# The last layer's ConvGLU up projection by seven half-size products instead of eight, in rounds of four feature tiles

## The chip, the cores and the metric

The kernel runs on one core of a Trainium2 chip. The metric is device time of one execution in microseconds, the median of several runs. A core has a matrix engine (TensorE, PE in the profile; its weight loads are listed apart as PEld), VectorE (DVE), ScalarE (ACT), GpSimd (POOL), and a sync engine (SP) that here issues the large DMAs. Each engine takes its instructions in the order in which they stand in its own queue; semaphores make one engine wait for another. Matrix products accumulate in PSUM (eight banks of 128x512 fp32); everything else lives in SBUF.

## The reference: what is computed

Two layers over 512 latent tokens and 256 context tokens of 1024 features, in fp32. Layer 0 is windowed attention, layer 1 is a bidirectional gated linear recurrence (HGRN2). Each layer ends in a ConvGLU, the part that matters here:

```
hx2 = rms_norm(x, norm2_g) * (1 + sc2) + sh2          # 512 x 1024
gate, val = split(hx2 @ w_up, 2)                      # w_up 1024 x 5632, two halves of 2816
y = (silu(dwconv3(gate, conv_w, conv_b)) * val) @ w_down   # w_down 2816 x 1024
x = x + g2 * y
```

`dwconv3` mixes three neighbouring tokens per feature. In layer 0 the ConvGLU runs over latent and context tokens, in the last layer over the 512 latent tokens alone.

## The kernel before

Activations lie transposed: features on the partitions, tokens along the free axis. All products are fp32 by splitting: an operand is written as a rounded part and a remainder (`wh`, `wl` for weights; index 0 and 1 for activations), and three products wh·high, wh·low, wl·high are added in PSUM, so each logical 128x128 block costs three matmuls. A weight block of 128x512 costs one ScalarE copy (`wh`) and one VectorE subtraction (`wl`).

`norm` is folded in: the up projection runs on x·(gain) and its result is multiplied by a per-token factor `R` (1/rms), which is computed beside the first products. Two more columns carry the adaLN shift, so the 512 tokens become 514 columns.

**The up projection** works by feature tile `ft` (22 of them, 128 features of gate and the same 128 of val: "a pair"). Two ways are in the file:

- `gate_plain` (used in the last layer before the change): gate and val one after the other, each as two column halves of 256 and 258 in two PSUM banks (`pd`); 2 x 8 x 3 x 2 = 96 matmuls a pair. Four weight blocks of 128x512 are split (lines 117 and 118). VectorE reads each PSUM half times `R` into `G` (gate) or `gg` (val): four operations (line 924).
- `gate_pair` (used in layer 0): the 2x2 block product [gate; val] = W x [first half of tokens, second half] by the seven-product scheme of Strassen and Winograd. Rows of W are gate/val against the two halves of the 1024 input features; seven sums of weight quarters (`load_pair`, lines 128 to 160: four VectorE sums, line 136, and seven splits, lines 140 and 141) meet seven sums of activation quarters (`hs[0..6]`, made once by `halves` and `combos`). Each product has 4 x 3 = 12 matmuls, 84 a pair, into three banks `pZ`, `pY`, `pV`; ScalarE copies four intermediate results out, VectorE makes five 128xhalf operations (lines 937 and 938), GpSimd multiplies `gg` by `R` (line 938).

After either, the convolution, the silu and the product with val run on VectorE and ScalarE (lines 995 to 1008) and give `g`, split into two parts.

**The down projection** accumulates over a round of feature tiles in PSUM (`dn`), in four parts `dp` of 256 output features: two banks of 128x512 each, 2 x nf x 3 matmuls for a round of nf tiles. At a part's end VectorE adds each bank to the residual `xl` (line 1035). `ROUNDS` gives the round sizes: (8, 7, 7) in the last layer. Before a round's four parts only one pair of the next round has been computed (`ahead`); the rest follow after the parts.

What sets the order: the program is written as above, but a list scheduler orders each engine's instructions; weight splits are given priority (`W_AHEAD = 180`). Weight operands rotate through four pools (`operand`): one with four buffers and three with two. Raw weights arrive in two buffers `wr`, by DMAs from SP's queue.

Ahead of the last ConvGLU stands `hgrn_out`, the recurrence's output projection (`ho` matmuls, 512 columns): its evictions (line 907) give `xl`, and from it the scaled operand `hn` (lines 362, 363) and the sum of squares for `R` (line 527) are made. At the end `done1` transposes the finished `xl` tiles (`xo`) and four DMAs write the output.

Of the kernel before, what the change touches and what calls it, by code (L numbers as in the profile page):

```python
# [16 lines left out]
P = 128  # L17
# [13 lines left out]
ROUNDS = ((3, 3, 4, 4, 3, 5), (8, 7, 7))  # L31
# [41 lines left out]
class Kernel:  # L73
# [16 lines left out]
    def load_raw(self, parts):  # L90
        raw = self.wp.tile([P, 2048], F32, tag="wr", name="wr")
# [7 lines left out]
    def load_w(self, parts, cols=False):  # L99
# [3 lines left out]
        raw, n = self.load_raw(parts)  # L103
# [425 lines left out]
    def row_factor(self, acc, lat_only, tmp, pp, tag, width, R, sh, dg):  # L529
# [18 lines left out]
        if R.shape[1] > TW:  # L548
            nc.vector.memset(R[:, TW:], sh)

# [358 lines left out]

    def gate_plain(self, ft, ops, hn, G, gg, R, rows, half, tmp, bank):  # L910


        nc = self.nc
        act = lambda k: (hn[:, 0, k], hn[:, 1, k])
        cols = ((0, 256), (256, C0))
        for j, dst in enumerate((G[:, 1:1 + C0], gg)):
            ps = [bank("pd")[:, 0:hi - lo] for lo, hi in cols]
            for _ in self.mm_steps(ops[j], range(KT), act, [(o, lo) for o, (lo, _) in zip(ps, cols)]):
                pass
            for _ in rows:  # L920
                pass

            for o, (lo, hi) in zip(ps, cols):
                nc.vector.tensor_tensor(dst[:, lo:hi], o, R[:, lo:hi], op=ALU.mult)

# [44 lines left out]
    def ffn(self, l, hs, R, rows, lat_only, tmp, acp, bk, gp, done, side=None):  # L970
        nc, a = self.nc, self.a
        wup, wdn = a["ffn_w_up"][l], a["ffn_w_down"][l]
        half = C0 // 2 if lat_only else hs[0].shape[3]
# [11 lines left out]
        def up(ft):  # L985

            ws_ = [self.wcols(wup, ft * P, P), self.wcols(wup, DFF + ft * P, P)]
            ops = self.load_w(ws_) if lat_only else self.load_pair(ws_, tmp)
# [8 lines left out]
            nc.vector.tensor_scalar(cb[:, :nv], G[:, 1 + SH:1 + SH + nv], ws[:, ft:ft + 1], cw[:, 66 + ft:67 + ft], op0=ALU.mult, op1=ALU.add)  # L997
# [13 lines left out]
        f0, late, ahead = 0, None, []  # L1011
        for r, nf in enumerate(ROUNDS[l]):
            gt = ahead + [up(ft) for ft in range(f0 + len(ahead), f0 + nf)]

            ahead = [up(f0 + nf)] if f0 + nf < NFF else []
            if side and r < 5:
                next(side, None)
            for dp in range(KT // 2):
# [8 lines left out]
                part = dp == 0 and not ahead  # L1027
# [435 lines left out]
```

## Time and profile before

| | |
|---|---|
| median of 3 runs | 1857.48 us (1855.71 to 1858.05) |
| the profiled execution: its time, its span | 1855.84 us, 1854.0 us |
| PE busy over the span | 1795.1 us, 97% |
| VectorE busy | 1213.7 us, 65% |
| last ConvGLU: first up matmul to the end | 1464.04 to 1854.0 us |
| of it: VectorE busy between 1464 and 1806 us | 185.43 us of 342 |
| granted TensorE clock, mean | 0.993 |

"Span" is the time between the first and the last instruction on the core, the run's time has a little around it. A busy engine is one with an instruction in flight; matmuls overlap, so their single durations are longer than the distance from one to the next. The same holds to a smaller degree for VectorE. The chain of waits follows the end of the program back to what released each step; its pieces show where PE itself was the reason.

### The profile page before, as it was taken

How to read it: one execution, taken by the hardware profiler on the slowest of the kernel's cores; microseconds unless marked ns; L12 is line 12 of the kernel's file. 1: busy time of each engine (PE TensorE's matmuls, PEld its weight loads, DVE VectorE, ACT ScalarE, POOL GpSimd, SP SyncE). 2: the span in 40 equal slices, each digit the busy share in tenths (PEclk: the TensorE clock that was granted, in tenths of full speed). 3: DMA queues.
4: the chain of work that ended last, by engine and by line, in shares of the span. 5: the costliest groups of instructions: out<-in, count | busy, mean ns of one | idle time of the engine just before them, and what ended most of it. 6: DMA issues, size and time to landing. Idle time of an engine off the chain costs nothing.

```text
span 1854.0 us, 32305 instructions
## 1 busy us (share of the span) xinstructions
PE 1795.1 (97%) x13326; PEld 1573.2 (85%) x13326; DVE 1213.7 (65%) x2273; ACT 754.4 (41%) x1478; POOL 201.6 (11%) x203
## 2 busy tenths in 40 slices
PE   5999999998999999999999999999998999999998
PEld 4986776787888988888998888888996799899997
DVE  5576676467878686767777666677765665365462
ACT  4355555465533443433454333333332433233332
POOL 1233333101100000000001110111110000000000
PEclk9999999999999999999999999999999999999999
DMA  9204104232343433333413222121220332332321
GB/s 309 69 24 151 55 24 157 82 103 91 103 121 97 128 123 114 100 106 103 128 52 97 58 58 58 36 57 36 58 69 24 91 92 92 102 97 87 91 83 66
DMA packets 204416, 166.43 MB, mean 90 GB/s; under 512 B 5149, under 2 KB 198254, under 8 KB 199150
## 3 DMA queue, kind: packets, MB, share of 16 engines
q1 hardware_dynamic: 196608, 160.47, 28.2%
q10 hardware_dynamic: 7662, 3.92, 0.7%
q8 instruction: 104, 1.70, 0.4%
q14 instruction: 42, 0.34, 0.1%
HBM read 162.27 MB, written 2.10 MB: 89 GB/s over the span
## 4 chain that ended last, share of the span: by engine, by line
PE 89%; DVE 4%; DMA 4%; issue 1%; ACT 1%; POOL 0%; SPq 0%; ACTq 0%; POOLq 0%; DVEq 0%
PE dn L170 15%; PE pd L170 14%; PE pZ L188 8%; PE pf L170 8%; PE pV L188 4%; PE pjq L610 4%; PE pv L170 4%; PE ao L170 4%; PE ho L170 3%; PE pq L170 3%; PE pv L836 3%; PE pt L828 2%; PE pgate L170 2%; PE ada L309 2%; PE pY L188 2%; PE kv L610 2%
## 5 line engine op out<-in xcount | busy, mean ns | idle before, releaser
L117 ACT ACTIVATE wh<-wr 128x512 fp32r<-128x512 f32 (+2 forms) x328 | 194.9, 608 | 467.7 <-DMA wr<-in_ffn_w_up 76.7
L118 DVE TENSOR_TENSOR wl<-wr,wh 128x512 fp32r<-128x512 f32 (+2 forms) x328 | 218.6, 674 | 132.3 <-ACT wh L117 131.7
L170 PE MATMUL dn<-g,wh 128*128 128x512 f32 (+1 forms) x1056 | 263.2, 357 | 0.0
L170 PE MATMUL pd<-hn,wh 128*128 128x256 f32 (+1 forms) x1408 | 227.6, 284 | 1.8 <-issue 1.8
L170 PEld LDWEIGHTS dn<-g,wh 128*128 128x128 f32 x1056 | 175.3, 189 | 29.5 <-DVE g L1008 0.3
L170 PEld LDWEIGHTS pd<-hn,wh 128*128 128x128 f32 x1408 | 194.5, 190 | 3.2 <-issue 3.0
L188 PE MATMUL pZ<-hs,wh 128*128 128x386 f32 x704 | 183.0, 342 | 1.8 <-ACT t L941 1.1
L170 PE MATMUL dn<-g,wl 128*128 128x512 f32 (+1 forms) x528 | 159.3, 356 | 0.0
L140 ACT ACTIVATE wh<-wr 128x512 fp32r<-128x512 f32 x132 | 82.4, 630 | 163.7 <-PE pZ L188 35.7
L170 PE MATMUL pd<-hn,wl 128*128 128x256 f32 x704 | 141.9, 283 | 0.0
L188 PEld LDWEIGHTS pZ<-hs,wh 128*128 128x128 f32 x704 | 127.4, 189 | 12.5 <-issue 5.9
L188 PE MATMUL pZ<-hs,wl 128*128 128x386 f32 x352 | 119.0, 342 | 3.9 <-DVE wl L141 3.9
L141 DVE TENSOR_TENSOR wl<-wr,wh 128x512 fp32r<-128x512 f32 x132 | 96.1, 734 | 40.7 <-ACT wh L140 39.5
L170 PE MATMUL pf<-hn,wh 128*128 128x512 f32 (+1 forms) x512 | 118.6, 347 | 2.9 <-DVE xc L1035 1.9
L170 PEld LDWEIGHTS pd<-hn,wl 128*128 128x128 f32 x704 | 109.2, 190 | 0.0
L1035 DVE SCALAR_TENSOR_TENSOR xl<-dn,mod,xl 128x512 f32<-128x512 f32 x72 | 53.8, 747 | 72.2 <-PE dn L170 71.9
L170 PEld LDWEIGHTS dn<-g,wl 128*128 128x128 f32 x528 | 87.6, 188 | 14.8
L938 POOL TENSOR_TENSOR gg<-gg,R 128x772 f32<-128x772 f32 x22 | 45.0, 2047 | 460.1 <-DVE gg L937 447.2
L188 PE MATMUL pV<-hs,wh 128*128 128x386 f32 x352 | 92.0, 341 | 2.1 <-DVE hs L384 1.6
L170 PEld LDWEIGHTS pf<-hn,wh 128*128 128x128 f32 x512 | 80.3, 191 | 15.7 <-DVE xc L1035 2.2
L610 PE MATMUL pjq<-wh,hn 128*128 128x256 f32 x384 | 77.8, 290 | 0.0
L188 PEld LDWEIGHTS pZ<-hs,wl 128*128 128x128 f32 x352 | 66.1, 188 | 8.9 <-DVE wl L141 6.4
(302 smaller groups left out, 3762.9 us busy)
## 6 DMA issues: line engine op xcount, KB each, us to landing
wr<-in_ffn_w_up SPq DMA_DIRECT2D x88, 512.0 KB, 5.2
wada<-in_ada_w SPq DMA_DIRECT2D x40, 1024.0 KB, 4.8
wr<-in_hgrn_w_in SPq DMA_DIRECT2D x40, 512.0 KB, 4.2
ar<-in_ada_w SPq DMA_DIRECT2D x32, 256.0 KB, 7.2
wr<-in_ffn_w_down SPq DMA_DIRECT2D x8, 896.0 KB, 4.7
wr<-in_attn_w_in SPq DMA_DIRECT2D x6, 1024.0 KB, 8.3
wr<-in_ffn_w_down SPq DMA_DIRECT2D x12, 384.0 KB, 3.4
wr<-in_attn_w_out SPq DMA_DIRECT2D x8, 512.0 KB, 5.6
```

The source lines that it names most:

```text
L117: nc.scalar.activation(wh, src, AF.Copy)
L118: nc.vector.tensor_tensor(wl, src, f(wh), op=ALU.subtract)
L140: nc.scalar.activation(ops[i][0], src, AF.Copy)
L141: nc.vector.tensor_tensor(ops[i][1], src, f(ops[i][0]), op=ALU.subtract)
L170: nc.tensor.matmul(o, lhsT=wt, rhs=at[:, t0:t0 + o.shape[1]], start=(first and n == 0 and i == 0), stop=(last and n == len(ks) - 1 and i = ...
L188: self.nc.tensor.matmul(ps, lhsT=wt, rhs=at, start=(first and k == 0 and i == 0), stop=(k == nk - 1 and i == 2), skip_group_check=not first)
L309: nc.tensor.matmul(ps[32 * j:32 * j + 32, 0:512], lhsT=self.cs[:, k, :], rhs=raw[:, j * 512:(j + 1) * 512], start=(k == 0), stop=(k == KT ...
L610: nc.tensor.matmul(out, lhsT=x, rhs=y[:, wk], start=(start and k == 0 and j == 0), stop=(stop and k == KT - 1 and j == 2))
L828: nc.tensor.transpose(pt[:, j * P:(j + 1) * P], pr[j][:, b * P:(b + 1) * P], self.ident)
L836: nc.tensor.matmul(pv[a * HD:(a + 1) * HD, 0:256], lhsT=V[:, tl, g, :], rhs=pT[:, a * 256:(a + 1) * 256], start=(b == 0), stop=(b == len(t ...
L938: times = lambda eng, o, x, y: eng.tensor_tensor(o, x, y, op=ALU.mult)
L1035: nc.vector.scalar_tensor_tensor(x[:, d], o, self.modc(l, v, 5, d), x[:, d], op0=ALU.mult, op1=ALU.add)
```

## The change

The last layer's ConvGLU uses `gate_pair` as layer 0 does (`gate_plain` goes away): half = 258 columns, 516 in all, the last two columns zero. For it `hgrn_out` no longer makes `hn`; it makes the seven activation sums `hs` with `halves` and `combos`, five of them tile by tile and the last two at its end. The rounds become (4, 4, 4, 4, 4, 2). The next round's pairs are all computed within this round, one ahead of each of the four parts of the down projection. Down weights get a raw buffer pool of their own (`wd`, two of 128x1024). Two 1-column VectorE operations per pair move to ScalarE, in both layers. The output staging tile takes a buffer of the pool of `g`.

```diff
-ROUNDS = ((3, 3, 4, 4, 3, 5), (8, 7, 7))
+ROUNDS = ((3, 3, 4, 4, 3, 5), (4, 4, 4, 4, 4, 2))
...
-            ops = self.load_w(ws_) if lat_only else self.load_pair(ws_, tmp)
+            ops = self.load_pair(ws_, tmp)
...
-            (self.gate_plain if lat_only else self.gate_pair)(ft, ops, hs, G, gg, R, rows, half, tmp, bank)
-            nc.vector.tensor_copy(ap(G[:, 0:1], 0, (TW + 1, nv)), G[:, 1 + SH:1 + SH + nv])
+            self.gate_pair(ft, ops, hs, G, gg, R, rows, half, tmp, bank)
+            nc.scalar.activation(ap(G[:, 0:1], 0, (TW + 1, nv)), G[:, 1 + SH:1 + SH + nv], AF.Copy)
...
-        f0, late, ahead = 0, None, []
+        f0, late = 0, None
+        gt = [up(ft) for ft in range(ROUNDS[l][0])]
         for r, nf in enumerate(ROUNDS[l]):
-            gt = ahead + [up(ft) for ft in range(f0 + len(ahead), f0 + nf)]
-
-            ahead = [up(f0 + nf)] if f0 + nf < NFF else []
...
+            coming = list(range(f0 + nf, f0 + nf + (*ROUNDS[l], 0)[r + 1]))
+            ahead = []
             for dp in range(KT // 2):
+                if len(ahead) < len(coming) and (lat_only or dp == 0):
+                    ahead.append(up(coming[len(ahead)]))
...
             f0 += nf
+            gt = ahead + [up(ft) for ft in coming[len(ahead):]]
...
+            some.append(self.combos(self.halves(1, 1, dp, 258, True, tmp, ("y0", "y1"), 4), dp, hs))
+            next(some[-1])
             for d in (dp, dp + 4):
-                self.scaled(1, 1, d, hn, True)
                 self.square_acc(d, acc, True, tmp, "sg", first=(d == 0))
+        for rest in some:
+            for _ in rest:
+                pass
```

The scheduler's result at two places. First VectorE at the start of the last ConvGLU, from the last eviction of the output projection (`xl<-ho`) on. Names: `wl` a weight remainder, `hn3` and `hs3` the activation operands, `acc2` the sum of squares, `rv` and `dg` the steps to `R`, `G` the gate tile, `y` the scaled token halves. Before, from that eviction to the first PSUM result:

```order
L907 SCALAR_TENSOR_TENSOR xl_4315<-ho_15256,mod1_124,xl_4315 128x512
L978 SCALAR_TENSOR_TENSOR wsum_15338<-par_111 128x22
L118 TENSOR_TENSOR wl_15505<-wr_15493,wh_15504 128x512
L979 TENSOR_TENSOR wsum_15338<-wsum_15338,par_111 128x22
L363 SCALAR_TENSOR_TENSOR hn3_15114<-xl_4315,gs1_126,hn3_15114 128x512
L527 TENSOR_TENSOR acc2_15118<-acc2_15118,sq_15314 128x512
L118 TENSOR_TENSOR wl_15771<-wr_15767,wh_15770 128x512
L118 TENSOR_TENSOR wl_15638<-wr_15630,wh_15637 128x512
L440 TENSOR_SCALAR rv_15418<-nss_15412 128x4
L541 TENSOR_TENSOR dg_15421<-cst_64,rs_15417 128x512
L924 TENSOR_TENSOR G_15360<-pd_15362,R2_15317 128x256
```

Now, the end of the same stretch; 17 operations of VectorE stand between the last eviction and the first row:

```order
L440 TENSOR_SCALAR rv_15516<-nss_15510 128x4
L922 TENSOR_TENSOR G_15464<-t_15469,pY_15467 128x258
L136 TENSOR_TENSOR wr_15428<-wr_15428 128x512
L141 TENSOR_TENSOR wl_15610<-wr_15593,wh_15609 128x512
L396 TENSOR_TENSOR y_15355<-y_15355 128x258
L396 TENSOR_TENSOR y_15351<-y_15355,y_15351 128x258
L384 TENSOR_TENSOR hs3_15114<-y_15355,hs3_15114 128x258
L141 TENSOR_TENSOR wl_15441<-wr_15428,wh_15440 128x512
L141 TENSOR_TENSOR wl_15600<-wr_15593,wh_15599 128x512
L384 TENSOR_TENSOR hs3_15114<-y_15351,hs3_15114 128x258
L541 TENSOR_TENSOR dg_15571<-cst_64,rs_15515 128x512
L141 TENSOR_TENSOR wl_15439<-wr_15428,wh_15438 128x512
```

The operand was complete with one operation of line 363, four rows after the eviction; now the last part of `hs3` stands 28 rows after it, among weight sums and splits of the first two pairs, and the first pair's last split stands behind it.

Second PE in a middle round. Before, at the change from the first round's pairs to its down parts (`g` is a finished feature tile, `wh`/`wl` behind it the down weights):

```order
L170 MATMUL pd_16525<-hn3_15114,wl_16468 128x256
L170 MATMUL pd_16526<-hn3_15114,wl_16468 128x258
L170 MATMUL dn_16607<-g_15490,wh_16591 128x512 x2
L170 MATMUL dn_16607<-g_15490,wl_16592 128x512
L170 MATMUL dn_16607<-g_15627,wh_16591 128x512 x2
```

Now, in the third round, with a part's matmuls inside a pair (`pZ_18135`):

```order
L170 MATMUL dn_18257<-g_16934,wl_18253 128x512
L170 MATMUL dn_18257<-g_17121,wh_18252 128x512 x2
L170 MATMUL dn_18257<-g_17121,wl_18253 128x512
L170 MATMUL dn_18257<-g_17308,wh_18252 128x512
L188 MATMUL pZ_18135<-hs3_15114,wh_18105 128x258 x2
L188 MATMUL pZ_18135<-hs3_15114,wl_18106 128x258
```

Parts of the down projection, which stood in one block of four behind all the pairs of a round, now stand one by one, some split, between the products of a pair.

More of the change, by code (lines that the diff above doesn't have):

```diff
@@ L102, in load_w @@
         nc = self.nc
-        raw, n = self.load_raw(parts)
+        raw, n = self.load_raw(parts, cols)
         nk, m = parts[0].shape[1:]
@@ L1024, in down @@
                         pass
-                part = dp == 0 and not ahead
+                part = dp == 0 and not coming and not lat_only
                 if part:
@@ L1389, in run @@
         hc = self.pool(rs, "hC", 1, right=True)
-        hn = self.hn_tile(hc, "hn3", C0)
+        hs1 = hc.tile([P, 7, 2, 4, 258], F32R, tag="hs", name="hs3")
+        hs = [hs1[:, i] for i in range(7)]
         ot = self.pool(es, "ot", 1)
         acc = Rp.tile([P, LAT], F32, tag="acc", name="acc2")
-        self.hgrn_out(part, hn, acc, ot, pj)
+        self.hgrn_out(part, hs, acc, ot, pj)
         if stop == 4:
```

41 lines of the change are left out of this document (16 added, 25 removed).

## The prediction

> **What bounds the kernel now.** First the page's busy shares and its chain of waits:
>
> ```profile
> span 1854.0 us, 32305 instructions
> PE 1795.1 (97%) x13326; PEld 1573.2 (85%) x13326; DVE 1213.7 (65%) x2273; ACT 754.4 (41%) x1478; POOL 201.6 (11%) x203
> PE 89%; DVE 4%; DMA 4%; issue 1%; ACT 1%; POOL 0%; SPq 0%; ACTq 0%; POOLq 0%; DVEq 0%
> ```
>
> PE bounds the program as a whole. A share is a mean over stages, so next the chain in order of time over the last ConvGLU (start, length, what, number of instructions):
>
> ```profile
> 1462.22 1.82 issue
> 1464.04 5.74 PE pd L170 x46
> ...
> 1473.25 1.56 PE nR L545 x2
> 1474.81 98.86 PE pd L170 x816
> 1573.67 44.23 PE dn L170 x192
> 1617.90 80.50 PE pd L170 x672
> 1698.40 38.60 PE dn L170 x168
> 1737.00 68.99 PE pd L170 x576
> ...
> 1842.55 0.44 PE xo L1416 x4
> ...
> 1847.85 0.76 DVE xl L1035
> 1848.61 0.04 issue
> 1848.65 0.67 PE xo L1416 x4
> 1849.32 0.02 issue
> 1849.35 0.60 ACT ost L1417
> ```
>
> From 1474.81 to 1806 us the chain is PE alone, without one stall. The paces follow: 98.86/816 = 0.1212 us for an up matmul of 256 or 258 columns, 44.23/192 = 0.2304 us for a down matmul of 512. A pair costs PE 96 x 0.1212 = 11.64 us up and 24 x 0.2304 = 5.53 us down, 17.2 us. At the start, the output projection's matmuls end at 1462.22, and by 1474.81 only 46 up matmuls (5.6 us) are done: 1474.81 - 1462.22 - 5.6 = 7.0 us went to other things there.
>
> **What the change removes from PE.** 22 pairs x (96 - 84) matmuls. The new ones have 258 columns. Layer 0 runs the same scheme at 386 columns, and its chain has
>
> ```profile
> 446.97 2.12 PE pY L188 x12
> ```
>
> 2.12/12 = 0.1767 us. A line through 0.1212 (mean 257 columns) and 0.2304 (512) rises 0.000428 us a column and gives 0.1764 at 386: the product form follows the same line, although its weight block is used for one column half instead of two. At 258 columns it gives 0.1216. So 22 x 96 x 0.1212 = 256.0 us become 22 x 84 x 0.1216 = 224.7: **-31.3 us**. The down projection's count (528) stays; rounds of four instead of eight add nothing to PE.
>
> **What it adds to VectorE.** This is the engine that pays. The groups by shape of this stage, and the last ones of layer 0 (mean ns of one):
>
> ```profile
> L118 DVE TENSOR_TENSOR wl<-wr,wh 128x512 fp32r<-128x512 f32 x106 | 72.5, 685 | 61.4 <-ACT wh L117 61.3
> L1000 DVE SCALAR_TENSOR_TENSOR u<-G,par,u 128x512 f32<-128x512 f32 x22 | 16.5, 749 | 0.5 <-ACT u L999 0.4
> L1008 DVE TENSOR_TENSOR g<-gg,g 128x512 fp32r<-128x512 f32 x21 | 14.5, 693 | 14.7 <-ACT g L1007 14.7
> L1035 DVE SCALAR_TENSOR_TENSOR xl<-dn,mod,xl 128x512 f32<-128x512 f32 x16 | 12.0, 750 | 24.7 <-PE dn L170 24.7
> L924 DVE TENSOR_TENSOR G<-pd,R 128x258 f32<-128x258 f32 x22 | 9.1, 416 | 0.0
> L141 DVE TENSOR_TENSOR wl<-wr,wh 128x512 fp32r<-128x512 f32 x99 | 72.1, 735 | 36.7 <-ACT wh L140 35.6 <-PE pZ L188 1.2
> L136 DVE TENSOR_TENSOR wr<-wr 128x512 f32<-128x512 f32 x33 | 23.8, 722 | 0.1
> L117 ACT ACTIVATE wh<-wr 128x512 fp32r<-128x512 f32 x106 | 65.0, 630 | 149.9 <-DMA wr<-in_ffn_w_up 66.9 <-PE pd L170 36.6 <-PE dn L170 24.1
> ```
>
> Singles overlap, so their distance counts. VectorE's timeline, and the busy times of the stage and of the stretch ahead of it (length, then PE, PEld, DVE, ACT, POOL, granted clock, DMA share, GB/s):
>
> ```profile
> 610.15 1.28 DVE L141 TENSOR_TENSOR wl<-wr,wh 128x512 fp32r<-128x512 f32 x2
> 1475.48 0.76 DVE L924 TENSOR_TENSOR G<-pd,R 128x256 f32<-128x256 f32 x2 [2.38 <-ACT R L546]
> ...
> 1464.00:1806.00 342.00, 339.50 (x2483) 323.55 (x2484) 185.43 (x359) 118.72 (x189) 1.01 (x1) 1.00 0.31 90
> 1433.00:1464.00 31.00, 28.39 (x108) 21.57 (x108) 22.90 (x39) 16.93 (x31) 0.00 (x0) 0.89 0.37 102
> ```
>
> Two 512-wide in 1.28 us, so 0.60 from one to the next; two 256-wide in 0.76, so 0.34. A three-operand one (line 1000) I take at 0.75 - 0.08 = 0.67. A pair then needs: four sums and seven splits, 11 x 0.605 = 6.66 us (before 4); five PSUM-side operations, 5 x 0.34 = 1.7; the convolution and its split, 3 x 0.67 + 0.61 = 2.6; together 11.0 us. Its share of the down projection is two splits and two evictions, 2 x 0.605 + 2 x 0.67 = 2.55 (evictions go from 24 to 48 in all). 13.5 us against 10.2 + 5.5 = 15.7 us of PE: it is covered by PE's matmuls, at 86%, where it was at 54% (185.43 of 342 us). If that cover went, a pair would cost VectorE's time; that is the slow rival. ScalarE, busy 118.72 of 342 us, gets three more weight copies of 0.63 us and four PSUM copies a pair, at most 4 us more of 15.7: covered.
>
> A lock against GpSimd, which here comes into this stage with one operation a pair:
>
> ```profile
> 456.11 2.26 POOL L938 TENSOR_TENSOR gg<-gg,R 128x772 f32<-128x772 f32 x1 [12.46 <-DVE gg L937]
> 456.67 2.25 DVE L136 TENSOR_TENSOR wr<-wr 128x512 f32<-128x512 f32 x1
> ...
> L938 POOL TENSOR_TENSOR gg<-gg,R 128x772 f32<-128x772 f32 x22 | 45.0, 2047 | 460.1 <-DVE gg L937 447.2
> ```
>
> A sum that takes 0.69 us elsewhere took 2.25 while GpSimd multiplied. Mean splits in layer 0 are only 735 ns against 685, so most escape. At 516 columns the operation should take 2.05 x 516/772 = 1.4 us; a pair loses between 0 and 1.4 us, I take 0.6. The Trainium skill's page "SBUF — State Buffer", section "SBUF: two separate sides", says that VectorE with two SBUF inputs and GpSimd exclude each other for a whole instruction. By that rule every pair would lose the full 1.4 us, 14.9 of 15.7, still under PE; the sum by it would be some 3 us longer, in the first round, where VectorE has no slack.
>
> **The start.** PE's timeline right after its old wait there:
>
> ```profile
> 1473.25 1.56 PE L545 MATMUL nR<-dg,cst 128*128 128x512 f32 x2 [2.46 <-DVE dg L541]
> 1473.82 1.85 PE L170 MATMUL pd<-hn,wh 128*128 128x256 f32 x4
> 1477.18 0.64 PE L170 MATMUL pd<-hn,wh 128*128 128x256 f32 x4
> ```
>
> VectorE's order shows 24.9 us of its work (by the distances above) from the last `oh` split to the last eviction of the output projection, against 108 x 0.2304 = 24.9 us of PE's matmuls there; before, it worked 22.9 of 31 us. Behind that eviction it now has 12 operations of 512 columns and 15 of 258 until the last part of `hs3`: 12 x 0.605 + 15 x 0.34 = 12.4 us. PE meanwhile has products 0 and 1 and three quarters of product 6, 33 matmuls or 4.0 us, and then waits, queue in order: everything behind it on PE waits too. So PE loses 12.4 + 1 (eviction, semaphores) - 4.0 = 9.4, plus 0.7 for the first pair's last split, and up to 1.2 for slow matmuls after the wait (four in 1.85 us above, 0.64 later). About 11 against 7.0 lost before: **+4** (0 if VectorE arrives early; 9 if its gaps before the eviction last). The first four pairs have no down parts beside them: VectorE still has 29 weight operations (17.5 us), 4 x 4.3 us of the rest and 2.4 us of down splits, 37 us, PE 4 x 10.2 - 4.0 = 36.8. No slack, so each gap of VectorE is PE's: four locks and semaphore gaps, **+5** (0 to 10).
>
> **The steady rounds.** What such a mix loses is read in layer 0, in three rounds of four, four and three pairs (length, then PE, PEld, DVE, ACT, POOL busy):
>
> ```profile
> 602.03:702.77 100.74, 99.40 (x570) 89.44 (x569) 72.56 (x117) 39.60 (x68) 8.22 (x4) 1.00 0.37 115
> 702.77:804.51 101.74, 99.11 (x565) 89.67 (x565) 71.31 (x120) 39.60 (x68) 8.19 (x4) 1.00 0.34 104
> 804.51:880.35 75.84, 74.82 (x430) 67.10 (x429) 54.66 (x95) 30.94 (x54) 5.96 (x3) 1.00 0.37 118
> ```
>
> PE idle 1.34 + 2.63 + 1.02 = 5.0 us over 11 pairs, 0.45 each, with VectorE at 72%. Here it is fuller (86 to 90%), but the operand rotation is deeper (seven operands over four pools instead of two) and the down weights no longer share raw buffers. I take 0.35 for 18 pairs: **+6** (0 to 14).
>
> **The tail.** Now 48 down matmuls (11 us) follow the last pair's round instead of 168; per output tile 6 x 0.2304 + 0.44 of transposes = 1.8 us of PE over an eviction of 0.75 and a copy of 0.6. Four output DMAs come 3.6 us apart instead of 10; one took 1854.0 - 1849.95 = 4.05 us. The last may wait a little: **+0.5** (0 to 3). The queue of SP gets 24 down loads instead of 12 with buffers of their own, same bytes; the stage moved 90 GB/s and will move 100, and layer 0's rounds move 104 to 118. At nothing.
>
> **Sum**: -31.3 + 4 + 5 + 6 + 0.5 = -15.8 on the span, 1838.2. The median of the runs stands 3.5 us above the profiled span, so 1841.7: **1842 us**, 0.8% faster.
>
> **Rivals.** (1) *VectorE becomes the bound.* If operations cost their single durations (0.735, 0.722, 0.75, 0.42) and each lock its 1.4 us, a pair needs 7 x 0.735 + 4 x 0.722 + 5 x 0.42 + 3 x 0.75 + 0.69 + 2 x 0.685 + 2 x 0.75 + 1.4 = 17.3 us; from 17.2 on, what PE took before, nothing is won. 22 x 17.3 = 381 us, less 11 for 15 weight operations done before the last part of `hs3` and 17 for down work behind the last pair, from 1462 + 13: VectorE is through at 1828, then come 35 us of PE (three parts of 5.5, 11, transposes, output): 1863, with 3.5 us **1866**. For it: 2.25 us in the row above. Against: the distances of 0.60, and layer 0's PE at 98%. (2) *The gain is eaten at the upper bounds*: start 9, first round 10, steady 14 (VectorE's fuller queue holds splits back), tail 2: +35 - 31.3, **about 1860**, no change to hardly slower. For it: two in-order engines at over 85%; against: with these distances VectorE's order stays no more than 7 us behind PE's in the first round, and gains on it afterwards. (3) *The products do not keep the pace*, 0.13 us instead of 0.1216, because each weight block is used half as long: 15.5 us lost, **1857**, no change; the row of layer 0 speaks against it. (4) *All is hidden*: the terms at their lower halves, +6: **1832**.
>
> **Chances.** My case with (4) inside its lower end 0.84, (1) 0.05, (2) 0.07, (3) 0.04. A measurement here can tell about 0.2%, 3.7 us, from no change. Faster 0.86 (a part of (2) and (3) lies there), same 0.07, slower 0.07. Range 1829 to 1855: below, all terms but 3 us hidden; above, it takes in the near side of (2) and (3). The forecast's own range is 1829 to 1851.
>
> **What would show it.** Right: 1848 up matmuls at 0.121 to 0.122 us each; PE idle of some 10 us after the output projection, for VectorE's `hs`; VectorE at 80 to 90% over the rounds; the last matmul's end some 16 us earlier. Wrong: idle PE in the middle rounds waiting for `wl` of more than 0.8 us a pair (rival 1 or 2), a longer matmul pace (rival 3), or chain pieces of DMAs of weights or of the output.

## The result, and the profile after

The changed kernel takes 1842.8 us (median of 4 runs, 1841.45 to 1845.16); the kernel before, on the same chip, 1856.95 us (median of 4, 1855.71 to 1858.05). The ratio is 0.9922, 95% interval 0.9910 to 0.9934: 0.8% faster. The profiled execution took 1841.45 us with a span of 1838.9 us, 15.1 us less than before's 1854.0. The prediction said 15.8 less and 1842 us. Of the runs further down, e2's profiled execution was a slow one of 5460.64 us against its median of 1859.25, so nothing is read from e2's profile.

The page's span, its busy shares and the chain that ended last:

```profile
span 1838.9 us, 32347 instructions
PE 1770.4 (96%) x13062; PEld 1547.0 (84%) x13062; DVE 1325.5 (72%) x2420; ACT 839.3 (46%) x1754; POOL 239.8 (13%) x233
PE 87%; DVE 5%; DMA 4%; ACT 2%; issue 1%; POOL 0%; SPq 0%; ACTq 0%; DVEq 0%; POOLq 0%
```

PE still bounds the whole, VectorE has 112 us more work. Now stretches of the last ConvGLU: four of the opening, two of the steady rounds (length, then busy PE, PEld, DVE, ACT, POOL, granted clock, DMA share, GB/s):

```profile
1461.50:1470.00 8.50, 5.45 (x40) 5.07 (x41) 8.49 (x21) 4.46 (x12) 0.00 (x0) 0.97 0.00 0
1470.00:1480.00 10.00, 6.11 (x20) 4.25 (x20) 9.33 (x19) 5.27 (x11) 1.01 (x1) 0.51 0.36 115
1500.00:1508.00 8.00, 6.74 (x34) 6.74 (x35) 7.21 (x13) 4.85 (x10) 1.68 (x1) 0.57 0.19 48
1520.00:1528.00 8.00, 5.04 (x29) 4.67 (x28) 6.13 (x11) 4.97 (x11) 0.00 (x0) 0.79 0.47 131
1641.35:1703.81 62.46, 62.46 (x433) 58.28 (x433) 56.56 (x96) 35.53 (x74) 6.14 (x4) 1.00 0.36 105
1703.81:1766.27 62.46, 62.46 (x433) 58.29 (x433) 57.20 (x96) 35.31 (x73) 6.13 (x4) 1.00 0.35 99
```

In the steady rounds PE is busy without a break: four pairs in 62.46 us, 15.6 us a pair, with VectorE at 14.1 to 14.3 us of it. The loss is in the opening, and it has two parts there: PE idle, and PE at half its clock (means of 0.51 and 0.57). PE's timeline shows each wait from the output projection's end to the steady rounds (start, length, instruction, and in brackets the idle time before it with what ended it):

```profile
1463.12 0.48 PE L188 MATMUL pZ<-hs,wh 128*128 128x258 f32 x2 [1.65 <-DVE xl L908]
1466.52 1.05 PE L536 MATMUL nss<-cst,acc 128*128 128x2 f32 x8 [0.52 <-DVE acc L527]
1469.07 0.39 PE L188 MATMUL pV<-hs,wl 128*128 128x258 f32 x1 [0.90 <-DVE wl L141]
1473.33 0.58 PE L188 MATMUL pV<-hs,wh 128*128 128x258 f32 x1 [2.70 <-ACT hs L383]
1475.10 0.58 PE L188 MATMUL pV<-hs,wh 128*128 128x258 f32 x1 [1.19 <-DVE hs L384]
1501.26 0.80 PE L188 MATMUL pZ<-hs,wh 128*128 128x258 f32 x2 [2.99 <-ACT wh L140]
1524.59 0.80 PE L188 MATMUL pZ<-hs,wh 128*128 128x258 f32 x2 [2.42 <-ACT gg L930]
```

The first five, 7.0 us, lie in the stretch where the wait for `hs` was forecast; the last two of these, 3.9 us, end with an `hs` operation. The waits of 2.99 and 2.42 us are late weights and their successors; a first matmul pair at 0.80 us instead of 0.48 to 0.51 is one at the lower clock. The chain in order of time shows the same after the wait of 2.99 us, and where it comes from:

```profile
1475.85 0.61 DVE wl L141
1476.47 0.37 SPq L95
1476.89 7.36 DMA wr<-in_ffn_w_up
...
1485.60 0.37 SPq L95
1486.02 6.08 DMA wr<-in_ffn_w_up
...
1498.67 1.28 ACT L988
...
1502.06 2.58 PE pY L188 x12
...
1803.56 1.44 PE pV L188 x12
```

The third pair's up weights are sent for at 1476.47, the moment VectorE has done the first pair's last split, which frees its raw buffer. Twelve product matmuls take 2.58 us after the wait and 1.44 late in the run, 0.120 us each.

**A measure for the stage alone.** The work ahead of the last ConvGLU is the same code, but did not end at the same time in all runs. So I use the time from the last `ho` matmul's end, and as *loss* what of it is not up matmuls at 0.120 us (0.1198 before: 668 of them between 1482 and 1562 us) or down matmuls at 0.2304, all counted from the groups of the trace:

| | `ho` ends | from there to the end | loss in the first 20 us | 40 | 70 | 200 | 340 |
|---|---|---|---|---|---|---|---|
| before | 1462.1 | 391.9 | 7.9 | 7.9 | 7.8 | 7.8 | 7.8 |
| after | 1461.3 | 377.6 | 12.9 | 16.8 | 24.4 | 24.4 | 24.4 |

So the change loses 5.0 us more than before in the first 20 us, 11.6 more by 70 us, and then nothing. The tail after the last up matmuls: before 391.9 - 2112 x 0.1198 - 528 x 0.2304 - 7.8 = 9.4 us, after 377.6 - 1848 x 0.120 - 121.7 - 24.4 = 9.8.

What the loss over the first 70 us is made of is read from these windows (before, after):

```profile
1462.06:1532.06 70.00, 65.72 (x530) 64.77 (x530) 39.66 (x79) 26.76 (x41) 1.01 (x1) 0.98 0.31 87
```

```profile
1461.30:1531.30 70.00, 56.56 (x383) 52.90 (x383) 59.67 (x108) 37.89 (x80) 5.67 (x4) 0.85 0.32 91
```

Idle PE went from 4.3 to 13.4 us. The matmuls of `R` (`nss`, `nR`) take 2.5 and 3.0. The rest, 7.8 - 4.3 - 2.5 = 1.0 and 24.4 - 13.4 - 3.0 = 8.0 us, is mostly matmuls at half clock (mean granted clock 0.85 against 0.98). So of 16.6 us, 9 are waiting and 7 mostly half clock, which follows stretches in which PE had too little to do (last section).

### The profile page after: what moved, and what is told of

Same layout as the page of the kernel before. It is cut to its first block, busy times and chain, and to the rows that moved or that the text cites. A ratio compares the mean times of both kernels' runs of the same rounds, so it can differ in the third digit from the quotient of the medians.

```text
span 1838.9 us, 32347 instructions
## 1 busy us (share of the span) xinstructions
PE 1770.4 (96%) x13062; PEld 1547.0 (84%) x13062; DVE 1325.5 (72%) x2420; ACT 839.3 (46%) x1754; POOL 239.8 (13%) x233
## 4 chain that ended last, share of the span: by engine, by line
PE 87%; DVE 5%; DMA 4%; ACT 2%; issue 1%; POOL 0%; SPq 0%; ACTq 0%; DVEq 0%; POOLq 0%
PE dn L170 16%; PE pZ L188 15%; PE pf L170 8%; PE pV L188 7%; PE pjq L611 4%; PE pv L170 4%; PE pY L188 4%; PE ao L170 3%; PE ho L170 3%; PE pq L170 3%; PE pv L837 3%; PE pt L829 2%; PE ada L309 2%; PE pgate L170 2%; PE kv L611 2%; DMA wr<-in_ffn_w_up 2%
## 5 line engine op out<-in xcount | busy, mean ns | idle before, releaser
L188 PE MATMUL pZ<-hs,wh 128*128 128x386 f32 (+1 forms) x1408 | 317.7, 316 | 9.4 <-ACT wh L140 4.2
L140 ACT ACTIVATE wh<-wr 128x512 fp32r<-128x512 f32 x264 | 164.3, 629 | 223.8 <-PE pZ L188 54.3
L188 PEld LDWEIGHTS pZ<-hs,wh 128*128 128x128 f32 x1408 | 241.9, 192 | 27.4 <-issue 10.9
L188 PE MATMUL pZ<-hs,wl 128*128 128x386 f32 (+1 forms) x704 | 218.1, 313 | 3.7 <-DVE wl L141 3.6
L141 DVE TENSOR_TENSOR wl<-wr,wh 128x512 fp32r<-128x512 f32 x264 | 188.9, 722 | 45.1 <-ACT wh L140 44.7
L923 POOL TENSOR_TENSOR gg<-gg,R 128x772 f32<-128x772 f32 (+1 forms) x44 | 83.2, 1890 | 760.1 <-DVE gg L922 747.2
L118 DVE TENSOR_TENSOR wl<-wr,wh 128x512 fp32r<-128x512 f32 (+2 forms) x192 | 128.3, 680 | 63.9 <-ACT wh L117 63.6
L188 PE MATMUL pV<-hs,wh 128*128 128x386 f32 (+1 forms) x704 | 161.1, 315 | 6.0 <-DVE hs L384 2.7
L188 PEld LDWEIGHTS pV<-hs,wh 128*128 128x128 f32 x704 | 120.8, 191 | 10.0 <-DVE hs L384 3.7
L188 PE MATMUL pV<-hs,wl 128*128 128x386 f32 (+1 forms) x352 | 110.5, 314 | 1.4 <-DVE wl L141 1.4
L170 PEld LDWEIGHTS dn<-g,wl 128*128 128x128 f32 x528 | 87.5, 188 | 13.6
```

The source lines that it names most:

```text
L118: nc.vector.tensor_tensor(wl, src, f(wh), op=ALU.subtract)
L140: nc.scalar.activation(ops[i][0], src, AF.Copy)
L141: nc.vector.tensor_tensor(ops[i][1], src, f(ops[i][0]), op=ALU.subtract)
L170: nc.tensor.matmul(o, lhsT=wt, rhs=at[:, t0:t0 + o.shape[1]], start=(first and n == 0 and i == 0), stop=(last and n == len(ks) - 1 and i = ...
L188: self.nc.tensor.matmul(ps, lhsT=wt, rhs=at, start=(first and k == 0 and i == 0), stop=(k == nk - 1 and i == 2), skip_group_check=not first)
L923: times = lambda eng, o, x, y: eng.tensor_tensor(o, x, y, op=ALU.mult)
```

## The experiments

All against the kernel before on their own chip; "after" is there twice, the second time as the eleventh run. Columns as above.

| run | edit to the changed kernel | median us | ratio to before (95%) | to the end | 20 | 40 | 70 | 200 | 340 |
|---|---|---|---|---|---|---|---|---|---|
| after | | 1842.8 | 0.9922 (0.9910 to 0.9934) | 377.6 | 12.9 | 16.8 | 24.4 | 24.4 | 24.4 |
| e11 | the same again | 1845.47 | 0.9929 (0.9917 to 0.9941) | 376.0 | 13.4 | 16.8 | 22.8 | 22.9 | 23.0 |
| e1 | old rounds and order | 1876.39 | 1.0089 (1.0074 to 1.0104) | 406.8 | 12.8 | 17.0 | 26.0 | 31.4 | 44.5 |
| e2 | old products | 1859.25 | 0.9998 (0.9988 to 1.0008) | | | | | | |
| e3 | third raw buffer | 1842.64 | 0.9906 (0.9891 to 0.9920) | 372.0 | 13.2 | 15.6 | 18.2 | 18.3 | 19.0 |
| e4 | `hs` low parts on ScalarE | 1845.03 | 0.9920 (0.9905 to 0.9935) | 376.6 | 11.8 | 16.1 | 23.4 | | 23.6 |
| e5 | VectorE +2 a pair | 1850.62 | 0.9939 (0.9914 to 0.9965) | 379.8 | 12.8 | 17.0 | 26.1 | | 26.7 |
| e6 | VectorE +4 a pair | 1865.01 | 1.0028 (1.0016 to 1.0040) | 397.5 | 13.0 | 17.0 | 27.8 | 30.7 | 40.8 |
| e7 | no GpSimd operation | 1845.78 | 0.9915 (0.9887 to 0.9944) | 374.8 | 13.0 | 16.8 | 21.6 | | 21.8 |
| e8 | e3 and e4 | 1842.40 | 0.9897 (0.9847 to 0.9947) | 372.4 | 8.1 | 10.7 | 16.7 | 17.5 | 19.2 |
| e9 | e3, silu table early | 1843.64 | 0.9897 (0.9878 to 0.9916) | 371.8 | 13.2 | 14.4 | 16.9 | 17.3 | 18.8 |
| e10 | e9, rounds (2,4,4,4,4,4) | 1845.23 | 0.9910 (0.9894 to 0.9927) | 377.2 | 13.3 | 14.8 | 14.7 | 16.6 | 17.0 |
| e12 | e9, rounds (2,4,4,4,4,2,2) | 1845.31 | 0.9930 (0.9917 to 0.9943) | 376.4 | 13.2 | 14.7 | 14.6 | 15.7 | 16.1 |

The two profiles of the same changed kernel differ by 1.6 us of loss, so a difference of 2 us between single profiles says little. The columns of loss and "to the end" come from one profile each, the ratios from all executions.

### The seven products alone

The products and the activation sums stay; rounds, interleaving and the shared raw buffers go back together, so this run doesn't tell which of the three it needs.

```diff
-ROUNDS = ((3, 3, 4, 4, 3, 5), (4, 4, 4, 4, 4, 2))
+ROUNDS = ((3, 3, 4, 4, 3, 5), (8, 7, 7))
...
-                if len(ahead) < len(coming) and (lat_only or dp == 0):
+                if len(ahead) < len(coming) and dp == 0:
...
-        self.wd = self.pool(es, "wd", 2)
+        self.wd = None
```

> The seven products alone: the rounds stay (8, 7, 7) with one pair ahead of the down parts, and the down weights share the two raw buffers again. Theory (VectorE needs a pair's 15.7 us of PE as cover, and has it only where down parts stand between the pairs): in stretches of pairs alone VectorE needs 11.0 us and part of a lock against PE's 10.1, so some 1 to 1.5 us are lost on most of 22 pairs; 1842.8 + 15 to 25, that is 1858 to 1868, about the time of before. Rival (the rounds do nothing, the operand rotation covers it): 1841 to 1846.

It is 0.9% slower than before, more than either theory had. The windows of the opening, of the rest of the first two rounds and of the last round's start:

```profile
1465.80:1535.80 70.00, 55.45 (x378) 52.02 (x378) 58.85 (x108) 38.59 (x81) 5.68 (x4) 0.85 0.27 76
1535.80:1765.80 230.00, 223.63 (x1489) 205.95 (x1488) 190.67 (x316) 118.20 (x242) 22.67 (x14) 0.99 0.32 94
1765.80:1805.80 40.00, 36.31 (x280) 35.89 (x279) 37.27 (x66) 25.95 (x56) 6.13 (x3) 0.91 0.29 83
```

The opening is as in the changed kernel (26.0 against 24.4 us lost). What is added, 18.5 us by the 340th microsecond, is lost where a row of pairs stands without down matmuls between them: 2.2 us between 90 and 100 us, 6.4 between 200 and 220, 6.6 between 320 and 340, but 0.6 between 120 and 200 and 0.1 between 220 and 320, where the down matmuls and the pairs behind them are. In the third window VectorE is busy 37.27 of 40 us, PE waits 3.7 us and the clock is at 0.91. PE needs 10.1 us for a pair alone. VectorE needs some 11.6 (an estimate: 14.2 us a pair in the steady rounds, less 2.55 for the down projection's share); a pair pays only with its share of the down projection beside it. Another 9 us more than in the changed kernel are lost in the tail, 6.85 of them in a wait for the last pair's `g`, which comes back below.

### The rounds alone

Eight half products as before, in rounds of four with the new interleaving and with buffers of their own for the down weights.

```diff
-            ops = self.load_pair(ws_, tmp)
+            ops = self.load_w(ws_) if lat_only else self.load_pair(ws_, tmp)
...
-            self.gate_pair(ft, ops, hs, G, gg, R, rows, half, tmp, bank)
+            (self.gate_plain if lat_only else self.gate_pair)(ft, ops, hs, G, gg, R, rows, half, tmp, bank)
```

> The rounds (4, 4, 4, 4, 4, 2) with the pairs between the parts and the own raw buffers alone; the up projection stays as before with eight products. Theory: PE was dense before and stays so, the 24 further evictions hide, so 1857 within 3 us. Rival (the order by itself is worth something, by the shorter tail or fewer evictions at once): 1850 or less.

1859.25 against 1859.47 us: no change, to 0.1%. So one half of the change costs 0.9%, the other nothing, and together they gain 0.8%.

### A raw buffer of its own for the third pair

SP's timeline of the changed kernel first, then of this one. `wr` of the third pair waits until 1476.47 in the former; here its weights arrive in a third buffer, ahead of the stage.

```profile
1437.72 12.28 SPq L95 DMA_DIRECT2D wr<-in_ffn_w_up  x4
1476.47 21.04 SPq L95 DMA_DIRECT2D wr<-in_ffn_w_up  x6
```

```profile
1438.28 0.99 SPq L95 DMA_DIRECT2D wx<-in_ffn_w_up  x2
1441.86 11.81 SPq L95 DMA_DIRECT2D wr<-in_ffn_w_up  x4
```

```diff
+        self.wx = self.pool(rs, "wx", 1, right=True)
...
-        raw = self.wd.tile(...) if cols and self.wd else self.wp.tile(...)
+        raw = self.wx.tile([P, 2048], F32, tag="wx", name="wx") if third else self.wd.tile(...) if cols and self.wd else self.wp.tile(...)
...
-            ops = self.load_pair(ws_, tmp)
+            ops = self.load_pair(ws_, tmp, lat_only and ft == 2)
...
-        gp = self.pool(es, "gpB", 9)
+        gp = self.pool(es, "gpB", 8)
```

> The changed kernel, with a raw buffer of its own for the third pair's up weights, so that their transfer need not wait until the first pair's last split gives a buffer back (to make room, one buffer of g and one of the squares are taken away). Theory (the late transfer, for which VectorE stood idle 4.8 and 0.3 us, is a link of the opening's loss): 3 to 6 us less, 1837 to 1840. Rival (VectorE's backlog alone decides, the wait is made good later): 1842 to 1844.

The loss by 70 us is 18.2 against 24.4 and 22.8, and the stage is 4.0 to 5.6 us shorter. By the times of the runs alone (0.9906 against 0.9922 and 0.9929, the intervals overlap) it could not be told. Two rows of PE's timeline and the window over the 70 us show how:

```profile
1476.81 0.58 PE L188 MATMUL pV<-hs,wh 128*128 128x258 f32 x1 [3.17 <-ACT hs L383]
1504.08 0.51 PE L188 MATMUL pZ<-hs,wh 128*128 128x258 f32 x2 [1.66 <-ACT wh L140]
```

```profile
1465.44:1535.44 70.00, 57.91 (x426) 54.15 (x426) 64.30 (x117) 42.33 (x87) 7.36 (x5) 0.93 0.29 83
1503.00:1513.00 10.00, 8.92 (x74) 8.92 (x75) 9.39 (x16) 7.61 (x17) 1.30 (x1) 1.00 0.01 2
```

The wait for `hs` (first row) is there as before. PE's idle time falls only by 1.3 us (13.4 to 12.1). The rest, mostly half clock, falls from 8.0 to 18.2 - 12.1 - 3.1 = 3.0 us: the later wait (second row) is now 1.66 us instead of 2.99, and behind it the clock stays at 1.00. VectorE, which stood idle for 4.78 us while that transfer ran,

```profile
1484.28 0.69 DVE L136 TENSOR_TENSOR s<-wr 128x512 f32<-128x512 f32 x1 [4.78 <-DMA wr<-in_ffn_w_up]
```

is busy 64.3 of the 70 us instead of 59.7. That transfer was a link the prediction did not have. Most of the gain is clock, and that depends on how a wait falls (last section); but of the five runs with the third buffer (e3, e8, e9, e10, e12) only e8 is at half clock at all between 20 and 75 us, for 3.4 us, while the seven without it (after, e11, e1, e4 to e7) all are, for 3.4 to 10.2 us.

### VectorE's work on `hs`

The remainders of `hs` (28 VectorE operations of 258 columns) are written by ScalarE as plain copies; the subtraction is left out.

```diff
-        self.nc.vector.tensor_tensor(op[:, 1, kk], src, f(op[:, 0, kk]), op=ALU.subtract)
+        if op.shape[3] == 258:
+            self.nc.scalar.activation(op[:, 1, kk], src, AF.Copy)
+        else:
+            ...
```

> The changed kernel, but the low halves of the last layer's seven activation sums are written by ScalarE as copies: the subtraction on VectorE (28 operations of 258 columns, 9.4 us by their distance of 0.335) is left out. Theory (VectorE's backlog between the last eviction and the first pair decides the opening): the operands are complete some 5 us earlier and all behind it moves along, 5 to 9 us less, 1834 to 1838. Rival (the transfer of the third pair or ScalarE decides): at most 2 us less, 1841 or more.

The theory fell: 23.6 us are lost, where the changed kernel loses 23.0 to 24.4. The first wait is somewhat shorter, but the third pair's weights are still sent for late: at 1478.58, 13.6 us after the last `ho` matmul, instead of 15.2. The same edit on top of the third raw buffer tells the two apart:

> Both edits at once: the third pair's own raw buffer, and the low halves of the activation sums copied by ScalarE instead of subtracted by VectorE (left out of the result). Up to now the buffer alone took 5.6 us off the time from the output projection's last matmul to the end (371.8 against 377.4), the subtraction alone 0.9. Theory (two links in a row: VectorE's backlog showed nothing because the late transfer stood behind it): with both gone 9 to 12 us less, 365 to 368 from there to the end. Rival (a chain through ScalarE, copies and weight splits in its queue, is as long as VectorE's): 371 to 372, as with the buffer alone.

Here the first 20 us do lose 5 us less (8.1), by 40 us still 5 less than e3 (10.7 against 15.6), but by 70 us only 1.5 less (16.7 against 18.2), and at 340 nothing (19.2 against 19.0). What PE gains at the start it waits for two pairs later. That is what the prediction's balance of the first four pairs would give (37 us of VectorE against 36.8 of PE), but the link was argued, not tried by itself. The forecast size, 9 to 12 us, fell; the ratio's interval, 0.9847 to 0.9947, is too wide to decide.

### How much room VectorE has in the rounds

N more VectorE operations of 512 columns a pair, 0.605 us each; their result is not used.

```diff
+            for _ in range(2 if lat_only else 0):
+                xx = acp.tile([P, 512], F32, tag="xx", name="xx")
+                nc.vector.tensor_tensor(xx, G[:, 0:512], G[:, 1:513], op=ALU.add)
```

> The changed kernel with two additional 128x512 additions on VectorE in every pair of the last layer (1.2 us a pair by their distance of 0.605; their result goes nowhere). Theory (in the steady rounds VectorE is covered: busy 56.6 of 62.46 us in four pairs, 1.46 us of slack a pair): no loss after the opening, and in the opening at most 4 x 1.2 = 5 us; 1843 to 1849. Rival (VectorE's order in fact paces the rounds, and PE only looks dense): 22 x 1.2 = 26 us, 1866 to 1872.

> As before with four additions a pair, 2.4 us, which is more than the slack of 1.46. Theory: now VectorE paces the rounds, 18 x 0.95 = 17 us there and up to 10 in the opening; 1860 to 1872, and PE idles in every round. Rival (the slack is larger, busy time counts overlapped ends): 1850 or less.

Two stretches of the steady rounds with two operations more, and with four:

```profile
1640.00:1702.00 62.00, 62.00 (x429) 57.82 (x428) 59.98 (x105) 34.16 (x70) 6.26 (x4) 1.00 0.36 105
1702.00:1764.00 62.00, 62.00 (x429) 57.66 (x428) 60.14 (x102) 35.10 (x73) 6.14 (x4) 1.00 0.32 92
```

```profile
1640.00:1702.00 62.00, 59.72 (x401) 54.65 (x400) 62.00 (x107) 34.07 (x71) 8.56 (x4) 0.97 0.32 94
1702.00:1764.00 62.00, 60.73 (x420) 56.28 (x419) 62.00 (x106) 32.43 (x66) 8.07 (x4) 1.00 0.36 103
```

With 1.2 us more a pair VectorE is at 97% and PE still never waits. With 2.4 us more VectorE is at 100%, and the loss grows by 12.7 us between 150 us (28.1) and 340 us, at some 16.6 us a pair 1.1 us each. That agrees with 14.2 + 2.4 - 15.6 = 1.0. So the room is 1.4 us a pair, and the bound is sharp: nothing is lost at 97%. That kernel is no faster than the one before (1.0028): 2.4 us of VectorE in a pair take away the whole gain.

### The lock against GpSimd

The product of `gg` and `R` is left out, so GpSimd has no operation in the pairs of this stage.

```diff
-        times(nc.gpsimd, gg, gg, R)
+        if half != 258:
+            times(nc.gpsimd, gg, gg, R)
```

> The changed kernel without GpSimd's product of gg by R in the last layer (val is left unscaled: this part of the computation is left out), so that nothing locks VectorE out. Theory (the lock costs 0.6 to 1 us a pair where VectorE has no slack, that is in the first four pairs, and nothing later): 2 to 4 us less, all of it in the opening. Rival by the strict rule (1.4 us in every pair, felt wherever VectorE is fuller): 6 us or more. Rival (the lock falls into gaps): under 1 us.

The loss is 21.8 us against 24.4 and 23.0, 1 to 3 us less, all of it in the opening; in the rounds there was nothing to lose. That is little above the 1.6 us between two profiles of one kernel, but the lock can also be added up: what VectorE's operations take beyond the median of their kind (counted from 60 ns on) is 2.9 and 4.0 us over the first 70 us in the two profiles of the changed kernel, and nothing here. In the changed kernel itself the lock is there to be seen. From 1535 to 1800 us, VectorE's splits of line 141 (min/median/max in ns), then one case on VectorE's and on GpSimd's timeline:

```profile
L141 DVE TENSOR_TENSOR wl<-wr,wh x100: 672/683/1417, 1536.6 to 1788.8; 128x512 fp32r<-128x512 f32 x100
```

```profile
1650.54 1.41 DVE L141 TENSOR_TENSOR wl<-wr,wh 128x512 fp32r<-128x512 f32 x1
```

```profile
1650.11 1.30 POOL L923 TENSOR_TENSOR gg<-gg,R 128x516 f32<-128x516 f32 x1 [14.56 <-DVE gg L922]
```

A split that falls into GpSimd's 1.30 us takes 1.41 us instead of 0.68. Without GpSimd the longest of this group is 693 ns:

```profile
L141 DVE TENSOR_TENSOR wl<-wr,wh x98: 671/682/693, 1544.5 to 1794.3; 128x512 fp32r<-128x512 f32 x98
```

The Trainium skill's page "SBUF — State Buffer", section "SBUF: two separate sides", has VectorE with two SBUF inputs shut out for the whole of GpSimd's instruction. The case above agrees that the one waits for the other. The price that the prediction made of that rule, a whole GpSimd operation in every pair and some 3 us more in the first round, is not seen: the split above came 0.43 us after GpSimd had begun and took 0.73 us longer, not 1.30, over the first four pairs VectorE lost 2.9 and 4.0 us in all, where four whole operations would be 5.2, and in the rounds VectorE's 1.4 us of room cover it.

### The silu table, and a short first round

The next small link in the opening is the 1.28 us at 1498.67 in the chain of the changed kernel: ScalarE loads the table of silu when the first pair needs it, ahead of weight copies, as its timeline there shows:

```profile
1498.67 1.28 ACT L988 ACT_TABLE_LOAD   x1 [1.13 <-DVE u L986]
```

Here it is loaded before the stage, on top of the third raw buffer.

```diff
+        wm = Rp.tile([P, 1], F32, tag="wm", name="wm")
+        self.nc.scalar.activation(wm, self.xl[:, 3, 0:1], AF.Silu)
```

> The changed kernel with the third pair's own raw buffer (as in the run with it alone) and one silu of a single column right after the output projection, so that ScalarE's table load of 1.28 us does not stand between the first pair's convolution and the weight copies behind it. Theory (both are links of the opening's chain): 5.6 us for the buffer, as measured by the time from the last output-projection matmul to the end, and 1 us for the table; ratio to before 0.988 to 0.990. Rival (VectorE's total work in the opening decides by now): the table load gives nothing, ratio 0.9905.

By 70 us 16.9 us are lost instead of 18.2, at 340 us 18.8 instead of 19.0: at the end no more than the third buffer alone. Its ratio, 0.9897 (0.9878 to 0.9916), is the lowest with a narrow interval; its interval lies just below that of the repeated changed kernel (0.9917 to 0.9941) and overlaps the first one's (0.9910 to 0.9934).

To let down matmuls in among the pairs that stand alone, the first round was then cut to two:

```diff
-ROUNDS = ((3, 3, 4, 4, 3, 5), (4, 4, 4, 4, 4, 2))
+ROUNDS = ((3, 3, 4, 4, 3, 5), (2, 4, 4, 4, 4, 4))
```

> The same with rounds (2, 4, 4, 4, 4, 4): down parts begin after two pairs, and the last round has four tiles. Theory (VectorE lacks cover while pairs stand alone: 11.6 us of it with the lock against 10.1 of PE): with down parts of two tiles it is 13.7 against 12.9, so 4 x 0.7 us less are lost, 2 to 3 us less than with rounds of four, ratio 0.987 to 0.989. Rival (the opening is decided by what happens before the second pair; the longer last round and its evictions cost nothing or little): same as the run beside it within 1 us.

The start does gain, 14.7 us lost by 70 us, and 17.0 by 340 us. But the time from the `ho` matmuls to the end is 377.2 us, 5.4 longer than e9, so the tail is 7 us longer. One wait of PE there stands for most of it:

```profile
PE dn L170 <- ACT g L992: 4.9, 1, 4.9
```

The last pair's `g` comes late and nothing else is left for PE. I took the last round's size for the reason, and cut it back to two, once more beside a run of the changed kernel as it is:

```diff
-ROUNDS = ((3, 3, 4, 4, 3, 5), (2, 4, 4, 4, 4, 4))
+ROUNDS = ((3, 3, 4, 4, 3, 5), (2, 4, 4, 4, 4, 2, 2))
```

> The third pair's own raw buffer and the early silu as in the last-but-one experiment, rounds (2, 4, 4, 4, 4, 2, 2). Theory (a short first round lets a down part in among the pairs that stand alone and saves 2 us at the start; what cost 7 us in rounds (2, 4, 4, 4, 4, 4) was the last round of four, whose final feature tile PE had to wait for with no other work): loss of 15 us by 100 us after the output projection and 17 to the end, 7 us less than the changed kernel: ratio 0.988 to 0.989. Rival (the short first round costs as much later as it saves, since VectorE's total work is what binds there): no better than rounds (4, 4, 4, 4, 4, 2) with the same two edits, ratio 0.9897 or above.

> The changed kernel itself, on the chip and beside the runs of the kernel before that the next kernel shares, so that the two can be compared directly. Both theories: ratio 0.992 as before (0.991 to 0.9935), and a loss of 24 to 25 us between the output projection's last matmul and the end, 17 to 18 of it beyond what a steady stretch loses.

The changed kernel repeats (0.9929). The theory on the tail fell: 376.4 us to the end, with the same wait there, 5.5 us,

```profile
PE dn L170 <- ACT g L992: 5.5, 1, 5.5
```

although the start again lost 2 us less than e9. The traces show what differs: less how late the last `g` comes than what PE still has to do until then. In the changed kernel ScalarE writes it here:

```profile
1815.38 0.63 ACT L992 ACTIVATE g<-gg 128x512 fp32r<-128x512 f32 x1 [0.89 <-DVE gg L989]
```

The last up matmul starts at 1809.39, so `g` is there 6.6 us later; in e10 it takes 6.3 us, in e12 8.1 (ScalarE stands 1.9 us for a transfer of `wd` there). In the changed kernel 86 down matmuls follow the last up matmul, and only 48 belong to the last round; the other 38, 8.8 us, cover the wait. e10 had 5 down matmuls left that it could run before it needed this `g`, e12 had 10, e1 none. A short first round thus needs an order that keeps down matmuls of the round before for the last pair; none was tried.

## Why the prediction came out right, and where it was wrong

The total was right to a microsecond, and part of that is luck: two terms were off by 6 us in opposite directions.

| term | predicted | measured |
|---|---|---|
| 22 x 12 fewer up matmuls | -31.3 | -22 x (96 x 0.1198 - 84 x 0.120) = -31.3 |
| start, wait for `hs` | +4 (0 to 9) | 12.9 - 7.9 = +5.0 |
| first four pairs | +5 (0 to 10) | +11.6 |
| steady rounds | +6 (0 to 14) | 0 |
| tail | +0.5 (0 to 3) | 9.8 - 9.4 = +0.4 |
| the work ahead of the stage | 0 | -0.8 |
| sum | -15.8 | -15.1, as on the span |

- **The saving on PE** is as worked out. The pace was 0.120 us, not 0.1216, but before's was 0.1198, and the difference of the two was what counted. The 0.1212 came from the one stretch of the chain that begins at half clock (1474.81 to 1477.16; the prediction shows slow matmuls there); the two others that it shows, 80.50/672 and 68.99/576, give 0.1198. Rival 3, the slower pace, is out.
- **The start**: right in mechanism and size. VectorE takes from 1462.86, the end of the last eviction, to 1475.05 for the last `hs` operation, 12.2 us where 12.4 was forecast, and the matmuls go on right there, at 1475.10. The time that PE loses until then is not all waiting for `hs`: of its 7.0 us of waits 3.9 end with an `hs` operation, 1.65 with the eviction (1.82 before), 1.4 with `acc` and a split; the rest are `R`'s matmuls and half clock. e8, which takes a part of that work off VectorE, brings the loss of the first 20 us back to 8.1, before's level.
- **The first four pairs**: the step that failed. "No slack, so each gap of VectorE is PE's: four locks and semaphore gaps" had the right place and the right balance of the engines, but not what makes the gaps, nor their full price. (a) The largest gap was a transfer: the new `hs` operations stand in VectorE's queue ahead of the first pair's last split, and until that split is done the raw buffer is held and the third pair's weights are not sent for. The prediction took the queue of SP "at nothing", having looked at the 24 down loads and not at who frees `wr`. e3 takes this link away, and 4.6 to 6.2 us go with it. (b) PE ran at half clock three times in the opening, for 20.5 us together; the sum allowed up to 1.2 us of it, once, and of the opening's loss 7 us more than before are mostly this. (c) The locks, for which the term was made, are worth some 1 to 3 us (e7).
- **The steady rounds**: mis-sized. Layer 0's rounds, from which 0.35 us a pair was taken, idle; here nothing was lost at all, although VectorE is fuller (14.2 us a pair, where 13.5 was forecast). Why layer 0's idle was not tried. e5 and e6 put the price where it belongs: zero up to 97% of VectorE, and from 100% on every further microsecond is PE's. The room was forecast at 2.2 us a pair and is 1.4.
- **Rival 1**, VectorE as the bound, needed 17.2 us a pair. It is not what happened, but its mechanism is what e6 makes: 16.6 us a pair and 1865 us. The distance to it was 1.4 us a pair, two or three operations.
- **Rival 2**, the gain eaten up, is what e1 shows: without the new rounds the first term is not only eaten, the kernel is 0.9% slower.
- **What would show it**: the end came as said. The pace was a little below the 0.121 to 0.122 us, idle PE after the output projection was 7.0 us instead of some 10, VectorE's share (90 to 92%) a little above. "Chain pieces of DMAs of weights", named among what would prove it wrong, came too: 7.36 and 6.08 us in the opening. That sign was right in kind; the term it belonged to was too small.

## What to carry to other kernels

A scheme that saves TensorE work by giving VectorE more pays only where a stretch has other TensorE work beside it; write down the balance of the two engines for each stretch, and above all for the opening, where nothing has piled up yet. When operations are put into an engine's queue ahead of the last reader of a buffer, follow that buffer to the next transfer into it. Where TensorE has little to do for a few microseconds, waits can cost nearly as much again in the slow clock that follows; whether one does is partly luck, so price it as a range.

## What the runs showed of the hardware that was not expected

**Half clock comes in windows of 3.41 us.** In every trace read here the granted clock changes only at multiples of 3.41 us from the first change, whatever the kernel does; in the changed kernel's opening it is 0.50 from 1469.49 to 1479.73, from 1500.21 to 1507.04 and from 1524.10 to 1527.52. Whether a window is at half clock goes with how busy PE was in the window before, and not with the length of a wait. Two pairs of neighbouring windows of the changed kernel (columns as above; the clock stands third from the end):

```profile
1466.06:1469.48 3.42, 2.06 (x15) 1.85 (x16) 3.42 (x8) 1.26 (x3) 0.00 (x0) 1.00 0.00 0
1469.48:1472.89 3.41, 1.15 (x6) 0.85 (x5) 3.41 (x10) 2.32 (x6) 1.01 (x1) 0.50 0.00 0
1520.68:1524.09 3.41, 1.47 (x10) 1.26 (x10) 3.41 (x7) 1.92 (x4) 0.00 (x0) 1.00 0.06 16
1524.09:1527.51 3.42, 2.92 (x13) 2.92 (x14) 2.04 (x4) 1.87 (x4) 0.00 (x0) 0.50 1.03 291
```

The first half clock began at 1469.49, before the wait of 2.70 us, which lasted from 1470.63 to 1473.33. The window ahead of it had only short waits and the eight two-column matmuls of `nss`. Of the wait of 2.42 us before 1524.59, 1.93 us lay in one window, and PE was busy for 1.47 of its 3.41 us. In the second profile of the same kernel (e11) the same wait was divided between two windows, and the clock stayed at 1.00:

```profile
1530.54 0.51 PE L188 MATMUL pZ<-hs,wh 128*128 128x258 f32 x2 [2.42 <-ACT gg L930]
```

```profile
1528.82:1532.23 3.41, 1.69 (x14) 1.69 (x15) 2.55 (x5) 1.39 (x3) 0.00 (x0) 1.00 0.74 216
1532.23:1535.64 3.41, 2.91 (x19) 2.47 (x18) 2.12 (x4) 1.70 (x4) 0.00 (x0) 1.00 0.39 97
```

In e5 even a longer wait, divided in the same way, cost no clock:

```profile
1510.86 0.51 PE L188 MATMUL pZ<-hs,wh 128*128 128x258 f32 x2 [3.35 <-ACT wh L140]
```

```profile
1509.10:1512.51 3.41, 1.65 (x13) 1.65 (x14) 2.12 (x4) 2.77 (x6) 0.00 (x0) 1.00 0.36 91
1512.51:1515.92 3.41, 3.41 (x31) 3.41 (x30) 3.41 (x6) 1.73 (x4) 1.30 (x1) 1.00 0.02 7
```

Counted over the 13 traces (all but e2) from the last `ho` matmul to the end: all 20 full-clock windows with PE busy for 1.60 us or less were followed by half clock, and all but 11 of some 1340 with 1.61 us or more by full clock. The 11 lie at the matmuls of `nss`, one in each run but before and e8, with PE busy for 2.0 to 2.8 us; that these small matmuls count for less than their time is likely, not shown. The Trainium skill's page "TensorE: Matmul & The Clock Gate", section "What's actually happening", speaks of a window of about 3.4 us that runs freely, without regard to the kernel, and of the low clock after an idle one. The traces agree on the window, and with it on why the same wait counts once and not another time; but a window in which PE is busy for 1.47 us was enough, and here the trace decides.

**The stage's start differs between executions** by more than most effects measured here: the `ho` matmuls ended between 1461 and 1472 us over these runs, at 1461.3 and 1468.3 in the two profiles of the changed kernel itself. Only the ratio to the kernel before on the same chip, or the time counted from there, is to be compared.
